# Row sums of an attention inverted and sent to DRAM: eight columns turned by the transfer in place of a turn on TensorE, with one large buffer fewer

## The chip, the core and the metric

The kernel runs on one core of a Trainium2 chip. Five engines work side by side, each through its own instructions in a fixed order: TensorE (PE in the profile, with its weight loads as PEld), VectorE (DVE), ScalarE (ACT), GpSimd (POOL) and SyncE (SP), which here does nothing but issue transfers. An engine waits at an instruction until the semaphores that it needs have been raised by others; what stands behind that instruction waits with it. Transfers (DMAs) between DRAM and the core's memory run beside all of them. The metric is the time of one execution in microseconds on the device.

## What is computed

Two layers of a hybrid encoder over 512 tokens of width 1024. Each layer has a half-step feed-forward block, a mixer and a second feed-forward block, each behind a norm that is shifted and scaled. The mixer holds two attentions, a pooling branch, three gates and an output product. The part that the change touches is the softmax of the two attentions:

```python
def chunked_relpos_attention(q, k, v, gq, gk, rel_bias):
    ...
    p = jax.nn.softmax(logits, axis=-1).astype(v.dtype)
    out = jnp.einsum('bhnqk,bnkhd->bnqhd', p, vb)
...
def forgetting_attention(q, k, v, gq, gk, f_logit):
    ...
        p = jax.nn.softmax(logits, axis=-1).astype(v.dtype)
        return jnp.einsum('bhqk,bkhd->bqhd', p, v)
```

Both have eight heads of 64 columns. The kernel leaves the division by the row sums of the softmax to the end: it weighs the values with the bare exponentials, and multiplies the result by the inverse row sums.

## The kernel before

All products are made in three passes of TensorE with each operand split in a high and a low part (`triple`, lines 119 to 121), so that weights are loaded by SP, split by ScalarE (`hi`, line 272) and VectorE (`lo`, line 274), and only then used.

The code is recorded in one pass. `pe[0]` counts the work given to TensorE so far, in units of a 512-column product; `later(delay, fn)` puts a step on a list that is due when the count has gone on by `delay`, and `poll()`, called before each triple, runs what is due. So the count decides where in the order a step stands. The recorded code then goes through a scheduler, which gives each engine its final order and gives each tile one of the buffers of its tag as these come free. The tag `b` has the largest pool: `NB` buffers of 4 KB in each partition, which serve the activations of the feed-forward blocks, raw weights (line 545), and in the mixer the queries, keys and outputs of the attentions.

`attention` runs for group "a" and then "c", in each of the two layers. Over the heads, four query blocks of 128 rows, taken in three groups:

- `logits` makes the logits in PSUM (line 1021, tag `mm`, four banks shared with other steps), VectorE adds the bias strip and takes the row maximum (line 1027), ScalarE takes the exponential with its row sum (line 1031) into column `odd * 4 + i` of a tile `sums` of 128 rows and 8 columns, one for a pair of heads.
- `turn` turns the exponentials (line 1052), `weigh` multiplies them with the values (line 1079) and adds the two halves into `rows_of[p][:, 0, :]` (lines 1082 and 1083), a `b` tile for each pair of heads whose rows are head columns and whose columns are tokens.
- `send` runs once for each pair, 20 units after the pair's last logits: VectorE inverts the sums (line 1088), TensorE turns the 128 x 8 tile to 8 x 128 (line 1090), ScalarE copies it out of PSUM (line 1092), and GpSimd's queue writes it to DRAM (line 1094), eight rows of 512 bytes.
- `spread`, 24 units later, reads it back with two transfers on GpSimd's queue, each a head's 512 inverse sums given to 64 partitions (line 1100), into `rows_of[p][:, 1, :]`.
- `norm_rows`, 40 units later, multiplies (line 1107) and splits the result for the branch product.

Between these steps a filler hands out triples of the projections or of the gates and branch products, so that TensorE has other work while an attention step waits. GpSimd also prepares the bias strips: a fill of a corner in "a" (line 993), an added mask in "c" (line 1004). There are four pairs, two groups and two layers, so `send` runs 16 times.

Of the kernel before, what the change touches and what calls it, by code (L numbers as in the profile page):

```python
# [15 lines left out]
F32 = mybir.dt.float32  # L16
# [6 lines left out]
P = 128  # L23
# [8 lines left out]
NT = T // P  # L32
# [8 lines left out]
def encoder_kernel(tc, xT, c, w_ada, b_ada, gains, w_gate, w_up, w_down, w_qkv, w_f, w_ubg,  # L41
                   qk_gain, rel, fbias, w_pool, pool_scale, w_branch, w_out, inv_cnt, w_first, out):
    nc = tc.nc
# [11 lines left out]

    mm = nc.tensor.matmul
    uid = [0]
    NB, NRAW = 17, 2

    def nm(s):  # L60
        uid[0] += 1
        return f"{s}_{uid[0]}"

    def st(shape, dt, tag, bufs):
        return sb.tile(shape, dt, tag=tag, bufs=bufs, name=nm(tag))
# [4 lines left out]
    def mmt(shape=(P, T)):  # L70
        return ps.tile(list(shape), F32, tag="mm", bufs=4, name=nm("mm"))
# [13 lines left out]
    pe = [0.0]  # L85
# [12 lines left out]
    def later(delay, fn, group=None):  # L98
        t = Task(pe[0] + delay, fn, group)
        tasks.append(t)  # L100
        return t
# [23 lines left out]
    ident = cp.tile([P, P], F32, name="ident")  # L125
# [49 lines left out]
    inv_dram = {(g, p): dr.tile([2 * NT, P], F32, name=f"inv_dram_{g}{p}") for g in "ac" for p in range(4)}  # L175
# [831 lines left out]
    def attention(qs, ks, vs, strip, ys, filler, budget, group):  # L1007
# [3 lines left out]
        sums, rows_of = {}, {}  # L1011

        def logits(h, group_, strips):
            p, odd = divmod(h, 2)
            (q, ql), k = qs[p], ks[p]
            s, lg, pr = mmt(), t1(T), t2(T)
            at = 0
            for i in group_:
                n = (i + 1) * P
                for z in (q, ql):  # L1020
                    mm(s[:, at:at + n], z[:, odd, i * P:(i + 1) * P], k[:, odd, :n], start=z is q, stop=z is ql)
                at += n
            at = 0
            for i in group_:
                n = (i + 1) * P
                mx = st([P, 1], F32, "mx", 4)
                nc.vector.tensor_tensor_reduce(out=lg[:, at:at + n], in0=s[:, at:at + n], in1=strips[i], scale=-1.0,
                                               scalar=BIG, op0=ALU.add, op1=ALU.min, accum_out=mx)
                if odd == 0 and i == 0:
                    sums[p] = st([P, 2 * NT], F32, "sm", 2)  # L1030
                nc.scalar.activation(pr[:, at:at + n], lg[:, at:at + n], AF.Exp, bias=mx, scale=-1.0,
                                     accum_out=sums[p][:, odd * NT + i:odd * NT + i + 1])
                pe[0] += 0.5 * (i + 1.5)
                at += n
            if odd and i == NT - 1:
                later(LAG_S, lambda: send(p), group)
            later(LAG_T, lambda: turn(h, group_, pr), group)
# [46 lines left out]
            pe[0] += 1.0 * nj  # L1084

        def send(p):
            rs = st([P, 2 * NT], F32, "rs", 1)
            nc.vector.reciprocal(rs, sums[p])
            tp = mmt()
            nc.tensor.transpose(tp[:2 * NT, :P], rs, ident)  # L1090
            flat = st([2 * NT, P], F32, "flat", 1)
            nc.scalar.copy(flat, tp[:2 * NT, :P])
            pe[0] += 0.5
            nc.gpsimd.dma_start(inv_dram[group, p], flat)
            later(LAG_R, lambda: spread(p), group)

        def spread(p):
            for off in range(2):
                r = inv_dram[group, p].rearrange("(h i) q -> h (i q)", h=2)[off:off + 1, :]
                nc.gpsimd.dma_start(rows_of[p][off * HD:(off + 1) * HD, 1, :], r.broadcast_to([HD, T]))  # L1100
            later(LAG_N, lambda: norm_rows(p), group)
# [293 lines left out]
```

## Time and profile before

| | us |
|---|---|
| median of three runs | 2376.86 (2376.07 to 2378.36) |
| the profiled execution, its own time | 2376.93 |
| its span, first to last instruction | 2375.2 |
| TensorE busy | 2356.4 |
| VectorE busy | 1781.1 |
| ScalarE busy | 1164.9 |
| GpSimd busy | 191.4 |

The granted TensorE clock is 1.00 throughout. The attentions run from about 445 to 655 us in the first layer and from about 1620 to 1832 us in the second. In the rows below, a row of the timeline has the start in us, the duration in us, the engine, the line of the code, the operation, the tiles (out<-in, buffer numbers left out), and in square brackets how long the engine stood idle before it and what ended the wait. A row of a group has the count behind an x and then shortest, median and longest duration in ns. A row of the waits has who waited, for whom, the total in us, how often, and the longest. The span of a busy TensorE is modelled: matmuls overlap, so their cost to the engine is the distance from one start to the next.

### The profile page before, as it was taken

The numbers are of one execution on the slowest core, as the hardware profiler recorded it, in microseconds if no ns is written. First come the engines' busy times: TensorE is split into PE (matmuls) and PEld (weight loads), VectorE is DVE, ScalarE is ACT, GpSimd is POOL, SyncE is SP. The second block draws the span as 40 slices with busy tenths as digits, with TensorE's granted clock in tenths as the row PEclk, the third lists the DMA queues.
The fourth block names the chain that finished last, engine by engine and source line by source line (L and its number), as shares of the span: only waits on it lengthen the run. The fifth ranks groups of instructions, "written<-read, shape, count | busy, mean of one in ns | idle before, by whom it ended". The sixth has DMA issues, their size and how long they took to land. (4 is left out here: it accounts for less than half of the span.)

```text
span 2375.2 us, 36712 instructions
## 1 busy us (share of the span) xinstructions
PE 2356.4 (99%) x14172; PEld 2092.2 (88%) x14172; DVE 1781.1 (75%) x3213; ACT 1164.9 (49%) x2048; POOL 191.4 (8%) x309
## 2 busy tenths in 40 slices
PE   8999999999999999999999999999999999999999
PEld 6899998788888898989998999888888888989998
DVE  8889866787668477788678778776866784767784
ACT  5354455676532353544554444556765324544452
POOL 2000002022120000000100000120222101000000
PEclk9999999999999999999999999999999999999999
DMA  7624432333458415244325334423243673223132
GB/s 274 223 91 162 140 128 95 95 98 123 127 188 289 152 63 193 99 143 148 110 89 187 117 115 133 160 89 99 87 138 112 235 258 133 89 98 124 64 116 89
DMA packets 118484, 325.19 MB, mean 137 GB/s; under 512 B 12034, under 2 KB 14338, under 8 KB 118308
## 3 DMA queue, kind: packets, MB, share of 16 engines
q1 hardware_dynamic: 115106, 314.38, 39.1%
q0 software_dynamic: 3200, 8.46, 1.0%
q8 instruction: 111, 1.82, 0.3%
q14 instruction: 65, 0.53, 0.1%
q10 hardware_dynamic: 2, 0.00, 0.0%
HBM read 316.35 MB, written 6.44 MB: 136 GB/s over the span
## 5 line engine op out<-in xcount | busy, mean ns | idle before, releaser
L272 ACT CAST whi<-raw 128x1024 fp32r<-128x1024 f32 (+1 forms) x260 | 270.1, 1043 | 322.4 <-PE acc L120 181.1
L274 DVE TENSOR_TENSOR wlo<-raw,whi 128x1024 fp32r<-128x1024 f32 (+1 forms) x254 | 309.9, 1224 | 156.3 <-ACT whi L272 154.3
L119 PE MATMUL acc<-b,whi 128*128 128x512 f32 (+1 forms) x704 | 262.3, 373 | 0.0
L121 PE MATMUL acc<-b,wlo 128*128 128x512 f32 (+1 forms) x704 | 260.5, 370 | 1.2 <-DVE wlo L274 1.2
L120 PE MATMUL acc<-b,whi 128*128 128x512 f32 (+1 forms) x704 | 260.8, 370 | 0.6 <-DVE b L383 0.6
L119 PE MATMUL mm<-b,whi 128*128 128x256 f32 (+1 forms) x768 | 244.7, 319 | 1.9 <-ACT t L586 1.7
L121 PE MATMUL mm<-b,wlo 128*128 128x256 f32 (+1 forms) x768 | 244.6, 318 | 0.0
L120 PE MATMUL mm<-b,whi 128*128 128x256 f32 (+1 forms) x768 | 244.5, 318 | 0.0
L198 DVE CUSTOM_DVE_ANT_0 v<-v,b,badac 128x1024 f32<-128x1024 f32 x144 | 187.5, 1311 | 20.2 <-DMA v<-in_w_ada_dram 19.9
L119 PE MATMUL mm<-hhi,whi 128*128 128x256 f32 (+1 forms) x616 | 198.8, 323 | 0.4 <-ACT t L586 0.4
L120 PE MATMUL mm<-hlo,whi 128*128 128x256 f32 (+1 forms) x616 | 199.1, 323 | 0.0
L121 PE MATMUL mm<-hhi,wlo 128*128 128x256 f32 (+1 forms) x616 | 199.0, 323 | 0.0
L120 PE MATMUL acc<-hlo,whi 128*128 128x512 f32 x480 | 188.1, 392 | 2.0 <-DVE hlo L790 1.8
L119 PE MATMUL acc<-hhi,whi 128*128 128x512 f32 x480 | 188.0, 396 | 1.0 <-ACT hhi L787 1.0
L121 PE MATMUL acc<-hhi,wlo 128*128 128x512 f32 x480 | 187.6, 391 | 0.0
L382 ACT CAST whi<-raw 128x1024 fp32r<-128x1024 f32 x96 | 100.7, 1049 | 121.3 <-PE mm L120 55.7
L119 PEld LDWEIGHTS mm<-b,whi 128*128 128x128 f32 x768 | 146.3, 190 | 12.4 <-ACT t L586 2.3
L120 PEld LDWEIGHTS mm<-b,whi 128*128 128x128 f32 x768 | 146.3, 191 | 10.3
L121 PEld LDWEIGHTS mm<-b,wlo 128*128 128x128 f32 x768 | 146.3, 190 | 10.2 <-DVE wlo L274 0.3
L121 PEld LDWEIGHTS acc<-b,wlo 128*128 128x128 f32 x704 | 132.6, 188 | 24.4 <-DVE wlo L274 1.6
L120 PEld LDWEIGHTS acc<-b,whi 128*128 128x128 f32 x704 | 132.7, 189 | 23.2 <-DVE b L383 1.4
L119 PEld LDWEIGHTS acc<-b,whi 128*128 128x128 f32 x704 | 132.7, 188 | 21.6
(326 smaller groups left out, 6112.8 us busy)
## 6 DMA issues: line engine op xcount, KB each, us to landing
v<-in_w_ada_dram SPq DMA_DIRECT2D x144, 512.0 KB, 4.8
raw<-in_w_down_dram SPq DMA_DIRECT2D x88, 512.0 KB, 3.8
raw<-in_w_up_dram SPq DMA_DIRECT2D x82, 512.0 KB, 3.6
b<-in_w_gate_dram SPq DMA_DIRECT2D x76, 512.0 KB, 6.3
raw<-in_w_ubg_dram SPq DMA_DIRECT2D x56, 512.0 KB, 4.1
raw<-in_w_qkv_dram SPq DMA_DIRECT2D x42, 512.0 KB, 3.7
raw<-in_w_branch_dram SPq DMA_DIRECT2D x24, 512.0 KB, 3.9
raw<-in_w_out_dram SPq DMA_DIRECT2D x16, 512.0 KB, 3.7
```

The source lines that it names most:

```text
L119: mm(o, lh, rh, start=start, stop=False, skip_group_check=onto)
L120: mm(o, lh, rl, start=False, stop=False, skip_group_check=onto)
L121: mm(o, ll, rh, start=False, stop=stop, skip_group_check=onto)
L198: dot = nc.vector.tensor_tensor_reduce(out=raw, in0=raw, in1=silc[0], scale=1.0, scalar=badac[:, l, j, d:d + 1], op0=ALU.mult, op1=ALU.add ...
L272: nc.scalar.copy(hi, raw)
L274: last["lo"] = lo_eng.tensor_tensor(lo, raw, hi.bitcast(F32), op=ALU.subtract).ins
L382: nc.scalar.copy(hi, src)
```

## The change

`send` no longer turns the tile on TensorE and copies it on ScalarE. The transfer reads the 128 x 8 tile as it is and writes each element to its turned place in DRAM, so that what lands there is the same 8 x 128 block. The tile `rs` has two buffers in place of one, the tile `flat` is gone, the count `pe[0]` no longer goes up by 0.5 in `send`, and the pool of `b` tiles has 16 buffers in place of 17.

```diff
-    NB, NRAW = 17, 2
+    NB, NRAW = 16, 2
...
         def send(p):
-            rs = st([P, 2 * NT], F32, "rs", 1)
+            rs = st([P, 2 * NT], F32, "rs", 2)
             nc.vector.reciprocal(rs, sums[p])
-            tp = mmt()
-            nc.tensor.transpose(tp[:2 * NT, :P], rs, ident)
-            flat = st([2 * NT, P], F32, "flat", 1)
-            nc.scalar.copy(flat, tp[:2 * NT, :P])
-            pe[0] += 0.5
-            nc.gpsimd.dma_start(inv_dram[group, p], flat)
+            with nc.allow_non_contiguous_dma(reason="128 x 8 inverse row sums, turned on their way"):
+                nc.gpsimd.dma_start(inv_dram[group, p].rearrange("j q -> q j"), rs)
             later(LAG_R, lambda: spread(p), group)
```

In the changed code the reciprocal keeps line 1088, the write has line 1090, and the spread has 1096 in place of 1100.

Three places in the orders. The first is TensorE at the first `send` of the first layer, as the difference of the two orders; `rs` is the tile of inverse sums, the `acc` rows are triples of the filler.

```order
 L120 MATMUL acc_4556<-wlo_4675,hhi 128x512
 L121 MATMUL acc_4556<-whi_4674,hlo 128x512
-L1090 MATMUL mm_4816<-ident,rs_4814 8x128
 L119 MATMUL acc_4556<-whi_4680,hhi 128x512
 L120 MATMUL acc_4556<-wlo_4681,hhi 128x512
```

One turn goes, and nothing comes in its place. From here to the end of each mixer's second attention the filler's triples stand one or two steps earlier or later among the attention steps than before; the rows themselves are the same but for the 16 turns.

The second is GpSimd at the last pair of group "a" in the first layer, before:

```order
L1004 TENSOR_TENSOR strip_5684<-strip_5684,cmask 128x128 x3
L1004 TENSOR_TENSOR strip_5870<-strip_5870,cmask 128x128 x3
L1094 DMA inv_dram_a_126<-flat_5764 8x128
L1100 DMA b_5608<-inv_dram_a_126 64x512 x2
L1004 TENSOR_TENSOR strip_5987<-strip_5987,cmask 128x128 x3
L1004 TENSOR_TENSOR ssum_5872<-ssum_5872,cmask 128x128
```

and of the change:

```order
L1004 TENSOR_TENSOR strip_5665<-strip_5665,cmask 128x128 x3
L1004 TENSOR_TENSOR strip_5839<-strip_5839,cmask 128x128 x3
L1090 DMA inv_dram_a_126<-rs_5734 128x8x1
L1004 TENSOR_TENSOR strip_5955<-strip_5955,cmask 128x128 x3
L1096 DMA b_5652<-inv_dram_a_126 64x512 x2
L1004 TENSOR_TENSOR ssum_5841<-ssum_5841,cmask 128x128
```

The three mask steps of a strip for a later head now stand between the write and the spread. On VectorE the multiplication of `norm_rows` for this pair (line 1107) has gone back behind the next two strips' steps of line 1027.

The third is VectorE at the first sum of `weigh` for the third pair of group "a" (heads 4 and 5), with buffer numbers. `b_912` before and `b_914` now are the same tile, `rows_of[2]`. Before:

```order
L289 SCALAR_TENSOR_TENSOR nt_u_895_5269<-nt_q_894_5268,nt_v32_892_5264 128x32
L1083 TENSOR_TENSOR b_912_5319<-mm_913_5320,t1_914_5325 64x256
L290 SCALAR_TENSOR_TENSOR nt_z_896_5270<-nt_u_895_5269,nt_j_893_5266 128x32
L1027 ISA t1_917_5332,mx_919_5338<-mm_916_5331,strip_915_5328 128x128
L1027 ISA mx_919_5338 128x1
```

and of the change:

```order
L1027 ISA t1_923_5372,mx_925_5376<-mm_922_5371,strip_908_5314 128x384
L1027 ISA mx_925_5376 128x1
L1060 TENSOR_TENSOR ptb_906_5304<-mm_921_5364,ptb_906_5304 128x4x128
L1060 TENSOR_TENSOR pta_926_5391<-mm_927_5392,pta_926_5391 128x384
L1083 TENSOR_TENSOR b_914_5330<-mm_915_5331,t1_916_5336 64x256
L1027 ISA t1_929_5402,mx_931_5406<-mm_928_5401,strip_908_5314 128x512
```

The sum has moved from before the first logits of head 5 to just before the last. In the changed program the tile stands in the buffer that held the queries of heads 4 and 5, and waits until the last logits that read them are made; before, it stood in a buffer whose last reader was done. The same holds for the first pair of group "c". On SP, the loads of raw gate weights (line 545) stand in six places behind one or two other loads that they stood ahead of, and in the attentions some strip loads and weight loads have changed places with the load next to them.

## The prediction

> **What bounds the kernel now.** I read the page first, then the windows, then TensorE's waits.
>
> ```profile
> PE 2356.4 (99%) x14172; PEld 2092.2 (88%) x14172; DVE 1781.1 (75%) x3213; ACT 1164.9 (49%) x2048; POOL 191.4 (8%) x309
> ```
>
> TensorE is busy for 2356.4 of 2375.2 us; no other engine comes near. The windows show where the missing 18.8 us are. A row has the window, its length, and the busy time of PE, PEld, DVE, ACT and POOL:
>
> ```profile
> 100.00:150.00 50.00, 50.00 (x336) 46.10 (x335) 49.49 (x76) 25.92 (x40) 0.00 (x0) 1.00 0.38 137
> 500.00:550.00 50.00, 49.29 (x275) 41.14 (x275) 42.33 (x103) 37.95 (x88) 8.28 (x18) 1.00 0.30 94
> 550.00:600.00 50.00, 49.67 (x277) 42.10 (x276) 33.93 (x74) 31.77 (x75) 13.83 (x27) 1.00 0.40 127
> 600.00:650.00 50.00, 49.84 (x274) 42.06 (x273) 31.43 (x68) 28.19 (x63) 9.90 (x22) 1.00 0.37 115
> ```
>
> A feed-forward stretch (the first row) leaves TensorE no idle time at all, and even the three windows of the first attention leave 0.71 + 0.33 + 0.16 = 1.2 us. So the change can gain two things: what TensorE itself spends on the 16 turns, and the few waits that hang on them. Everything off TensorE counts only if it makes TensorE wait. Of all TensorE's waits two belong to `send`:
>
> ```profile
> PE mm L1021 <- ACT flat L1092: 0.7, 2, 0.3
> PE mm L1090 <- DVE b L925: 0.5, 2, 0.2
> ```
>
> In the first, the logits wait for the PSUM bank that the copy to `flat` still holds; in the second the turn itself waits for a bank.
>
> **The turns on TensorE.** One turn takes 270 ns by its own row, but these spans overlap, so I take the distances of the starts:
>
> ```profile
> L1090 PE MATMUL mm<-ident,rs x16: 269/270/273, 473.9 to 1821.6; 128*8 128x128 f32 x16
> 473.67 0.39 PE L121 MATMUL acc<-whi,hlo 128*128 128x512 f32 x1
> 473.90 0.27 PE L1090 MATMUL mm<-ident,rs 128*8 128x128 f32 x1
> 473.93 0.48 PE L119 MATMUL acc<-whi,hhi 128*128 128x512 f32 x1
> 474.24 0.40 PE L120 MATMUL acc<-wlo,hhi 128*128 128x512 f32 x1
> 474.47 0.39 PE L121 MATMUL acc<-whi,hlo 128*128 128x512 f32 x1
> ```
>
> A triple's product starts 0.23 us after the one before (474.24 to 474.47). From 473.67 to 474.24 stand two products and the turn: 0.57 - 0.46 = 0.11 us for the turn. Sixteen of them are 1.8 us. The two waits above, 0.7 + 0.5 = 1.2 us, lose their cause. The next in line for those logits is VectorE, which reads them; I see no row that says it is late there, so I count both in full. Together **-3.0 us**.
>
> ScalarE loses 16 copies of some 0.25 us (4 us in all); it is half idle, and nothing on TensorE is gained by it beyond the bank just counted.
>
> **The write, element by element.** The trace has no transfer of 1024 single elements. The nearest ones, all on GpSimd's queue:
>
> ```profile
> L1094 POOL DMA_DIRECT2D inv_dram_a<-flat x8: 512/512/538, 475.5 to 1729.3; - x8
> DMA to landing us min/median/max: 1.5/2.0/3.1
> L1230 POOL DMA_DIRECT2D x_dram<-xv x8: 563/572/711, 351.2 to 1550.0; - x8
> DMA to landing us min/median/max: 2.9/3.1/3.9
> q0 software_dynamic: 3200, 8.46, 1.0%
> ```
>
> The issue takes 512 ns for 8 rows and 572 ns for the 128 rows of `x_dram`: 0.5 ns a row, so about 1.0 us for 1024 pieces; were it all in proportion to the rows, 8 x 0.57 = 4.6 us. For the landing, the lower end is the 1.5 us of the same 4 KB in eight rows. For the upper end I use the queue's packets: 1.0% of 16 engines' 2375 us is 380 us for 3200 packets, 0.119 us each at 2.6 KB on average; 64 pieces for each of 16 engines would take 7.6 us, on top of 3.1. So 1.5 to 10.7 us; I take **4 us**, nearer the lower end, because the bytes are those of the eight-row write.
>
> The plainest rule against this change is in the Trainium skill, "DMA: Bandwidth & Descriptors", section "Rules for kernel authors": a plain transfer with a rearranged access pattern is no way to turn data, 19 times slower than the chip's own transposing transfer. No run here shows that factor. Taken as 19 times the 2.0 us of the eight-row write it would be an estimate of 38 us, and sixteen of them would come to hundreds of microseconds of late norms.
>
> What hides it is the way from the reciprocal to the norm. The tightest case is the last pair of group "a":
>
> ```profile
> 549.42 0.20 DVE L1088 RECIPROCAL rs<-sm 128x8 f32<-128x8 f32 x1
> 551.68 0.25 ACT L1092 COPY flat<-mm 8x128 f32<-8x128 f32 x1
> 550.43 2.36 POOL L1004 TENSOR_TENSOR strip<-strip,cmask 128x128 f32<-128x128 f32 x3 [8.19 <-DVE b L925]
> 552.75 0.51 POOL L1094 DMA_DIRECT2D inv_dram_a<-flat  x1
> 555.95 1.08 POOL L1100 DMA_DIRECT2D b<-inv_dram_a  x2 [2.69 <-DMA inv_dram_a<-flat]
> 557.84 1.62 POOL L1004 TENSOR_TENSOR strip<-strip,cmask 128x128 f32<-128x128 f32 x3 [0.81 <-DMA strip<-fv_dram]
> 560.89 0.86 DVE L1107 TENSOR_TENSOR b<-b 128x512 f32<-128x512 f32 x1 [1.17 <-DMA b<-inv_dram_a]
> 564.55 0.55 DVE L1027 CUSTOM_DVE_ANT_0 t<-mm,strip 128x384 f32<-128x384 f32 x1
> ```
>
> The sums are inverted at 549.6, yet the write went at 552.75, partly because it waited for the turn and the copy, partly because GpSimd was at a strip until 552.79. In the new order the write still follows that strip, so here it starts no earlier; elsewhere, as at the first pair, it gains what lay between reciprocal and copy (some 3 to 4 us). Behind it now stand the three mask steps, which ran until 557.84 + 1.62 = 559.46 because their strip had to land first. The spread follows at 559.5 in place of 555.95, so **the write may take 559.5 - 552.8 = 6.7 us before it is late by itself**. The spread took 4.9 us to the norm's start, so the norm could start at 564.4. It stands behind line 1027's steps of about 562.6 now, so VectorE waits there about 1.8 us, and the logits' step of 564.55 slips to about 565.1, half a microsecond. VectorE waited before, too:
>
> ```profile
>   DMA b<-inv_dram_c: 8.2, 2
>   DMA b<-inv_dram_a: 1.9, 2
> ```
>
> These are the four waits of line 1107 for the spread, up to 4.1 us each, and among TensorE's waits none names that line. I therefore price half a microsecond of slip on VectorE at nothing on TensorE; without that cover it is 0.5 us in each layer, 1.0 in all.
>
> **Sixteen buffers.** In the feed-forward blocks the loads of raw gate weights are the ones that must now wait for an older tile. The tightest:
>
> ```profile
> 108.71 1.60 SPq L545 DMA_DIRECT2D b<-in_w_gate_dram  x2
> 109.56 0.39 PE L121 MATMUL mm<-b,wlo 128*128 128x512 f32 x1
> 113.56 1.05 ACT L382 CAST ptb<-b 128x1024 fp32r<-128x1024 f32 x1 [0.49 <-DMA b<-in_w_gate_dram]
> 114.99 1.22 DVE L383 TENSOR_TENSOR ptb<-b,ptb 128x1024 fp32r<-128x1024 f32 x1
> 121.38 0.28 PE L119 MATMUL acc<-hhi,ptb 128*128 128x256 f32 x1
> ```
>
> It was issued at 108.71; now it waits for the product that ends at 109.95, 1.24 us later. The cast and the subtraction behind it end at 116.21 and slip to about 117.5, and TensorE needs them at 121.38. The largest slip is that of a load that was issued early:
>
> ```profile
> 192.07 0.90 SPq L545 DMA_DIRECT2D b<-in_w_gate_dram  x2
> 205.15 0.33 SPq L545 DMA_DIRECT2D b<-in_w_gate_dram  x1
> 217.16 1.05 ACT L382 CAST ptb<-b 128x1024 fp32r<-128x1024 f32 x1 [1.05 <-PE acc L121]
> b<-in_w_gate_dram SPq DMA_DIRECT2D x76, 512.0 KB, 6.3
> ```
>
> The second of the two at 192 must now wait for the same step as the one at 205.15, about 12.5 us; with 6.3 us to land it is there by 212, and its first reader runs at 217.16. Its place on SP is now behind two loads that were waiting in the same stretch anyway. Cost: nothing, with 3.9 us to spare at the tightest.
>
> In the attention the third pair's first sum, and that of the first pair of "c", now wait for queries that are still read:
>
> ```profile
> 515.72 0.41 DVE L1083 TENSOR_TENSOR b<-mm,t 64x256 f32<-64x256 f32 x1
> 523.07 0.69 PE L1021 MATMUL mm<-b,b 128*128 128x512 f32 x2
> 525.42 0.27 PE L1052 MATMUL mm<-ident,t 128*128 128x128 f32 x1
> ```
>
> The sum ran at 515.72; now it must wait for the last logits of head 5, which end at 523.76, and ends at 524.2 at the earliest. Until then it holds one of the four PSUM banks and one of two `t1` tiles. The next user of that bank in the new order is the turn that ran at 525.42: about 1.2 us to spare. Queued behind the sum on VectorE is the last strip of the same head, which needs those very logits. So I price it at nothing; if VectorE runs late there, TensorE waits what is missing, and I allow 2 us for each of the four places, 8 us in all.
>
> **Other order.** The filler's triples have moved by one or two. At best all TensorE's idle time of the attentions goes: 2 x 1.2 us, of which 1.2 is counted already, so another -1.2.
>
> **The sum.** The profiled execution took 2376.93 us (span 2375.2), the same as the median 2376.86 within 0.1. 2376.9 - 1.8 - 1.2 = **2373.9 us**, 0.13% faster. About 0.2% (4.8 us) is what a measurement of this kernel can tell from no change: below 2372.1 is faster, above 2381.7 slower.
>
> **The rivals.**
>
> *Nothing is gained, or the banks take it back.* The two waits pass to another release, or the sums that wait for their buffer cost TensorE about what the turns cost it. For it: only 1.2 us to spare at 525.42. Against it: the filler stands between, and the scheduler has put the sum where its buffer comes free. 2376 to 2380, say 2377.
>
> *The element-wise write is the new wait (slower).* The place is the norm on VectorE, in order ahead of the logits' steps; the point is a landing later than 6.7 us. For it: the upper bound is 10.7. Against it: the bytes are few, and VectorE's waits of 4.1 us cost TensorE nothing visible. At 10.7 us the norm is 4.0 us late; if that falls on half of the sixteen sends, 32 us of VectorE's time, and VectorE is busy for 72% of the three windows above (107.7 of 150), TensorE loses 0.72 x 32 = 23 us: 2397. At a landing of 8.5 us it is 10 us: 2384. The Trainium skill's rule on rearranged patterns (above) is this same mechanism taken much further: a landing of 38 us would be 31 us late on all sixteen, an estimate of 360 us. I see nothing in the rows that comes near it, and give it 1 in 100 of this rival's chance.
>
> *The new order suits better.* The idle rest goes as well and a few waits shorter than the rows show: 2373.9 - 1.2 = 2372.7, and with the spread of runs (1 us) just under 2372. For it: the waits exist; against it: there is so little idle time that the order has almost nothing to give.
>
> **How the numbers follow.** Forecast 0.42; nothing gained 0.22; the write late 0.20; the better order 0.16. The better order counts as faster with most of its chance, and the forecast lends a little: 0.18 faster. The write late, with the larger part of the 8 us of the banks: 0.22 slower. Same: 0.60. The range reaches from a little under the better order, 2370.5, to 2386, which holds the write up to a landing of nearly 9 us.
>
> **What would show it.** The turn's line gone from TensorE, its total 1.8 us less busy, and the two rows gone from its waits: the gain. The write's landing in the DMA part: below 6.7 us right, above it a rival. Line 1107's waits for the spread: longer than 10.1 us in all, but without TensorE behind them. TensorE's idle time in 500 to 650 us: about 0.6 us less each layer; if it grows, and line 1052 or 1021 waits for line 1083, it is the buffers. A feed-forward window under 50.00 would prove the load term wrong.

## The result, and the profile after

The changed kernel takes 2449.8 us (2448.7 to 2451.0, four runs) against 2377.6 for the kernel before: a ratio of 1.0304, with an interval of 1.0292 to 1.0316. That is 72 us slower, where 3 us faster was forecast, and far outside the range of 2370.5 to 2386.

The first lines of the page, and windows of the first layer, three of the attention and one of the feed-forward block ahead of it, to set beside those of before (columns as there: the window, its length, busy time of PE, PEld, DVE, ACT and POOL, granted clock, DMA share, GB/s):

```profile
span 2448.7 us, 36723 instructions
PE 2376.4 (97%) x14156; PEld 2103.9 (86%) x14156; DVE 1778.2 (73%) x3213; ACT 1158.5 (47%) x2032; POOL 195.5 (8%) x309
...
500.00:550.00 50.00, 47.66 (x261) 39.48 (x260) 38.79 (x94) 33.98 (x78) 9.14 (x18) 1.00 0.38 93
550.00:600.00 50.00, 41.09 (x223) 34.20 (x222) 27.25 (x66) 25.08 (x62) 12.04 (x21) 0.93 0.39 101
600.00:650.00 50.00, 43.26 (x222) 36.65 (x221) 27.79 (x62) 25.97 (x61) 8.36 (x16) 0.90 0.32 88
100.00:150.00 50.00, 50.00 (x336) 46.08 (x335) 49.30 (x76) 25.77 (x40) 0.00 (x0) 1.00 0.41 137
```

Two things are new. TensorE stands idle for 2448.7 - 2376.4 = 72.3 us, where it was 18.8 before. And it is busy for 20 us more although 16 instructions are gone: the clock that was 1.00 throughout has fallen to 0.90 in the third of these windows. In the fourth, the feed-forward one, TensorE is busy for all of its 50 us, as before: the loads of raw gate weights, which have a buffer fewer, cost it nothing there.

The waits of TensorE and VectorE, the longest rows that were not there before or were much shorter (who waited, for whom, total, times, longest):

```profile
PE mm L1021 <- DVE mx L1027: 30.5, 7, 6.7
PE mm L1052 <- DVE mx L1027: 10.1, 2, 5.7
DVE b L1103 <- DMA b<-inv_dram_c: 65.1, 8, 10.2
DVE b L1103 <- DMA b<-inv_dram_a: 26.1, 7, 9.3
```

Line 1103 (1107 before) is the norm's multiplication. VectorE stands there for 91.2 us, at 15 of the 16 pairs; before it was 10.1 us at four. Behind it in VectorE's order stand the logits' steps of line 1027, and TensorE waits for those.

One pair from end to end, the third of group "c" in the second layer, in the timeline:

```profile
1821.92 0.20 DVE L1088 RECIPROCAL rs<-sm 128x8 f32<-128x8 f32 x1 [0.42 <-ACT t L1031]
1824.05 0.92 POOL L1090 DMA_DIRECT2D inv_dram_c<-rs  x1
1834.91 1.05 POOL L1096 DMA_DIRECT2D b<-inv_dram_c  x2 [9.22 <-DMA inv_dram_c<-rs]
1843.07 0.69 DVE L1103 TENSOR_TENSOR b<-b 128x512 f32<-128x512 f32 x1 [8.98 <-DMA b<-inv_dram_c]
1844.49 1.01 PE L1021 MATMUL mm<-b,b 128*128 128x384 f32 x2 [5.47 <-DVE mx L1027]
1845.30 0.63 PE L119 MATMUL acc<-b,whi 128*128 128x512 f32 x1
1845.72 0.63 PE L120 MATMUL acc<-b,whi 128*128 128x512 f32 x1
1846.15 0.63 PE L121 MATMUL acc<-b,wlo 128*128 128x512 f32 x1
```

The write is issued at 1824.05 and the spread can follow only at 1834.91. It needs another 8.2 us to the norm. VectorE has stood for 8.98 us by then and TensorE for 5.47, and the products that come next start 0.42 us apart, not 0.23. The windows of the same stretch show why:

```profile
1826.00:1834.00 8.00, 8.00 (x45) 6.80 (x44) 6.05 (x11) 5.25 (x10) 0.00 (x0) 1.00 0.11 12
1836.00:1842.00 6.00, 3.02 (x18) 2.34 (x16) 0.00 (x0) 0.00 (x0) 1.26 (x3) 1.00 0.99 288
1843.00:1846.00 3.00, 1.51 (x4) 1.42 (x5) 2.22 (x7) 1.85 (x7) 0.47 (x1) 0.50 0.00 0
```

While the write is on its way, **all transfers together move 12 GB/s**. Weight loads are issued into this window at 1828.14 and 1831.68, and one of them lands 10.9 us after its issue. Then what was held up comes at once, at 288 GB/s, and the spread has to share with it. When TensorE can go on, its clock is granted at 0.50.

The landing of the write (first line below), of the spread (second), and of the weight loads of line 261 between 545 and 690 us (third), each as shortest, median and longest:

```profile
DMA to landing us min/median/max: 9.7/11.1/11.6
DMA to landing us min/median/max: 3.0/6.0/7.5
DMA to landing us min/median/max: 3.5/6.2/9.0
```

Before they were 1.5/2.0/3.1, 2.7/3.2/5.7 and 3.4/3.9/4.5. Yet the transfer engines do little for the write. GpSimd's queue has as many packets as before, and its share has gone from 1.0% to

```profile
q0 software_dynamic: 3200, 8.46, 1.4%
```

which is 34 in place of 24 us for each engine (1.4% of 2449, 1.0% of 2375). The write of the pair above is 16 packets of 256 bytes in the trace, 0.40 to 0.49 us each, and all of them are over by 1826.4. In the 4.6 us from there on no packet of any queue starts (second row):

```profile
1825.60:1826.40 0.80, 0.80 (x6) 0.62 (x5) 0.43 (x1) 0.78 (x2) 0.09 (x1) 1.00 0.59 5
1826.40:1831.00 4.60, 4.60 (x26) 3.90 (x25) 3.65 (x6) 3.19 (x6) 0.00 (x0) 1.00 0.00 0
```

So most of the 10 us come behind the packets, in a time for which the profile counts no work of these engines.

### The profile page after: what moved, and what is told of

The parts are those of the page before. It is cut to its first block, busy times and chain, and to the rows that moved or that the text cites. A ratio compares the mean times of both kernels' runs of the same rounds, so it can differ in the third digit from the quotient of the medians.

```text
span 2448.7 us, 36723 instructions
## 1 busy us (share of the span) xinstructions
PE 2376.4 (97%) x14156; PEld 2103.9 (86%) x14156; DVE 1778.2 (73%) x3213; ACT 1158.5 (47%) x2032; POOL 195.5 (8%) x309
## 4 chain that ended last, share of the span: by engine, by line
PE 80%; DMA 8%; DVE 5%; issue 3%; ACT 3%; POOL 2%; DVEq 0%; SPq 0%; ACTq 0%; POOLq 0%
PE acc L119 16%; PE acc L120 16%; PE acc L121 16%; PE mm L119 10%; PE mm L121 10%; PE mm L120 10%; DMA b<-inv_dram_c 2%; DMA inv_dram_a<-rs 1%; DMA b<-inv_dram_a 1%; DMA inv_dram_c<-rs 1%; PE mm L1021 1%; POOL strip L1141 1%; ACT whi L272 1%; PE mm L1079 1%; DVE v L198 1%
## 5 line engine op out<-in xcount | busy, mean ns | idle before, releaser
L119 PE MATMUL acc<-b,whi 128*128 128x512 f32 (+1 forms) x704 | 265.1, 377 | 0.2 <-ACT b L382 0.2
L120 PE MATMUL acc<-b,whi 128*128 128x512 f32 (+1 forms) x704 | 264.3, 375 | 0.2 <-DVE b L383 0.2
```

Of the source, the lines that this page charges most:

```text
L119: mm(o, lh, rh, start=start, stop=False, skip_group_check=onto)
L120: mm(o, lh, rl, start=False, stop=False, skip_group_check=onto)
```

## The experiments

### The buffers: the change with 17, and before with 16

```diff
-    NB, NRAW = 16, 2
+    NB, NRAW = 17, 2
```

in the change, and the reverse in the kernel before.

> The change with 17 buffers of tag b kept. Theory L (the element-wise write makes its own pair late: it lands after some 11 us, the spread and the norm come late, VectorE stands at the norm with the next logits behind it): about 2450 us, within 5 of the changed kernel. Theory S (the write holds up every other transfer for some 10 us, so that strips and weights are late as well as the spread): the same, about 2450. Theory B (the sixteenth buffer and the order that it brings are what cost): 2374 to 2380.

> The kernel before, turn and copy kept, with 16 buffers of tag b. Theories L and S: within 4 us of before, as the prediction priced the buffers at nothing with up to 8 us allowed. Theory B: most of the 72 us, 2430 or more.

The change with 17 buffers took 2428.4 us, 1.0207 (1.0186 to 1.0228) of before; the kernel before with 16 took 2379.9, 1.0002 (0.9992 to 1.0013). Sixteen buffers cost nothing by themselves, and theory B falls. But with the element-wise write the 17 buffers are 21 us better, which no theory expected: the write lands in 9.9 us by the median, and VectorE waits at the norm for 57.6 + 21.2 us in place of 91.2. The order differs between the two in many places, so this may be the place where a stop of the transfers falls and not the buffer; which of the two was not tried.

### A write that nobody waits for, in three forms

The kernel before, with one more write behind each norm, read by nothing. Its turn, copy and eight-row write are untouched. First with single elements, dense in DRAM:

```diff
             split_to(y[:, 0, :], y[:, 1, :], full)
+            with nc.allow_non_contiguous_dma(reason="read by nothing"):
+                nc.gpsimd.dma_start(spare[group, p].rearrange("j q -> q j"), y[:, 0, :2 * NT].bitcast(F32))
```

> The kernel before with one more element-wise write of 128 x 8 to turned places for each of the 16 pairs, into DRAM that nobody reads, from the norm's result, so that it starts when its own pair's chain is done. Theory L: nothing waits for these writes, so 2376 to 2383. Theory S: the transfers of all queues move next to nothing for about 9 us behind each of them, the strip and weight loads issued then land 5 to 9 us later than in before, and the time rises by 20 to 70 us: 2397 to 2447.

Then the control, the same 4 KB as eight rows:

```diff
+            nc.gpsimd.dma_start(spare[group, p], y[:2 * NT, 0, :P].bitcast(F32))
```

> The control for the spare write: the same place, the same tile, the same 4 KB, but as 8 rows of 512 bytes. Theory S (the single elements stop the other transfers): 2376 to 2384, loads land in their usual 3.5 to 4.5 us. Theory Q (GpSimd's queue pays, because its instruction waits for the norm's result with the strips and the next pair's write behind it): the 52 us of the spare element-wise write come again, 2420 to 2435.

And last, when the forms below had been seen, the same 1024 elements with 64 bytes from one to the next (theories G and N are told with the forms: G has elements that share a line of 64 bytes written one after the other, N has the number of pieces count):

```diff
+                nc.gpsimd.dma_start(spare[group, p][:, :, 0].rearrange("j q -> q j"), y[:, 0, :2 * NT].bitcast(F32))
```

> The spare write of single elements again, from the same place and tile, but with 64 bytes from one element to the next in DRAM: as many pieces, none beside another. Theory G: a stop of some 3 us in place of 9, which the loads' lead mostly covers: 2380 to 2395. Theory N: as the dense spare write, 2425 to 2440.

| spare write | us | ratio to before (interval) | its landing, us |
|---|---|---|---|
| 1024 elements, dense | 2431.7 | 1.0217 (1.0202 to 1.0233) | 9.4/10.1/12.2 |
| 8 rows of 512 bytes | 2379.9 | 1.0000 (0.9990 to 1.0010) | 1.5/2.0/4.4 |
| 1024 elements, 64 bytes apart | 2376.6 | 0.9998 (0.9989 to 1.0007) | 3.0/3.4/4.5 |

Dense elements cost 52 us though nothing waits for them. The control excludes GpSimd's queue (theory Q): the instruction stands at the same place and waits for the same tile, and in all three kernels the other instructions of every engine stand in the same order as before. The third row has as many elements and the same issue time (0.92 us), and is free. Its 16 packets take as long as those of the dense write (0.49 us at most in both); behind the last of them it lands within 0.7 to 1.5 us, and the dense write, where its landing could be read, 6.0 to 8.4 us later. The window from about 4 to 8 us behind the first spare write, in the kernels with dense elements, with rows, and with elements apart:

```profile
494.50:498.50 4.00, 4.00 (x27) 3.48 (x26) 2.83 (x7) 2.76 (x8) 2.51 (x4) 1.00 0.14 15
494.60:498.60 4.00, 4.00 (x27) 3.48 (x25) 2.84 (x7) 2.77 (x8) 1.79 (x3) 1.00 0.48 152
496.20:500.20 4.00, 4.00 (x27) 3.49 (x26) 2.82 (x7) 2.76 (x8) 2.50 (x4) 1.00 0.50 144
```

The same loads are due at this place in all three: 15 GB/s in the first, 144 to 152 in the others. In the dense version TensorE waits behind VectorE and for weights, and VectorE for spreads that a stop holds up though their own write has eight rows:

```profile
PE mm L1022 <- DVE ptb L1061: 20.9, 11, 4.3
PE acc L119 <- ACT whi L273: 8.6, 4, 4.5
DVE b L1108 <- DMA b<-inv_dram_c: 43.7, 8, 6.8
```

This is theory S: the write stops the transfers of others. In the changed kernel the write also stands in its own pair's chain, as theory L has it; how the 72 us divide between the two was not measured.

### The change with a write that is not turned

```diff
-                nc.gpsimd.dma_start(inv_dram[group, p].rearrange("j q -> q j"), rs)
+                nc.gpsimd.dma_start(inv_dram[group, p].rearrange("j (a b) -> (j a) b", b=2 * NT), rs)
```

> The change with its 4 KB written as they lie, 128 rows of 32 bytes one behind the other, not turned (so the inverse sums that are read back belong to other rows). All else is the change. If the forecast's sum without the write is right (1.8 us of turns and 1.2 us of waits off TensorE): 3 us under before, about 2374 to 2377 where before is at 2377 to 2380. If the 16 buffers or the order cost something in the change: 2382 or more. If the wait for a write from 128 rows is a cost by itself: over 2390.

It took 2375.6 us, 0.9992 (0.9982 to 1.0001) of before. The instructions of all engines stand in the same order as in the change, so its profile is the change without the stop:

```profile
span 2371.5 us, 36723 instructions
PE 2353.0 (99%) x14156; PEld 2091.5 (88%) x14156; DVE 1777.9 (75%) x3213; ACT 1160.0 (49%) x2032; POOL 191.4 (8%) x309
DMA to landing us min/median/max: 1.7/1.8/3.5
DVE b L1103 <- DMA b<-inv_dram_a: 4.7, 2, 2.4
```

The third line is the landing of the write of 128 rows, the fourth VectorE's waits at the norm. Against the change the span is 2448.7 - 2371.5 = 77.2 us shorter. TensorE's idle time is 18.5 in place of 72.3 us, 53.8 less, and its busy time 2353.0 in place of 2376.4, 23.4 less for the same instructions: **the dense elements cost 54 us of waiting and 23 us of lower clock**.

### The norm later, and the write on another queue

```diff
-    LAG_T, LAG_V, LAG_S, LAG_R, LAG_N = 30, 20, 20, 24, 40
+    LAG_T, LAG_V, LAG_S, LAG_R, LAG_N = 30, 20, 20, 24, 80
```

> The change with the norm recorded 40 units (about 9 us) later, so that VectorE meets it when the spread has landed. Theory L: nearly all is regained, 2376 to 2395 (the last pair of each group is fetched early by the branch product and stays late). Theory S: the norm's waits go, but strips and weights still land late: 2400 to 2440.

2430.1 us, 1.0200 (1.0182 to 1.0218). It agrees with theory S by its number, but it is no test: the scheduler put the norm back to the same place in VectorE's order (two of the 16 stand one step earlier), and VectorE still waited there for 56.2 + 18.3 us. As with the 17 buffers, some 20 us are gained with small changes in the order of every engine; which of them gains it is open.

```diff
-                nc.gpsimd.dma_start(inv_dram[group, p].rearrange("j q -> q j"), rs)
+                nc.sync.dma_start(inv_dram[group, p].rearrange("j q -> q j"), rs)
```

> The change with its element-wise write issued by SP in place of GpSimd. If the stop comes from the single elements, whoever issues them: the other transfers stop for 9 us again, 2430 to 2460. If it comes from the way GpSimd's queue makes its descriptors: the write lands in 2 to 4 us, and the time is 2372 to 2385.

2405.8 us, 1.0110 (1.0091 to 1.0129): between the two that were expected. The write on SP's queue lands after

```profile
DMA to landing us min/median/max: 8.3/8.7/10.9
```

and the stop is there: below, the same weight load in this kernel, issued 1.7 us behind such a write, and in the one whose write is not turned, each for 6 us from about 1.3 us behind the load's issue.

```profile
530.00:536.00 6.00, 6.00 (x31) 5.00 (x31) 4.49 (x12) 3.77 (x11) 0.00 (x0) 1.00 0.21 29
527.80:533.80 6.00, 6.00 (x31) 5.02 (x31) 4.50 (x13) 3.76 (x11) 0.52 (x2) 1.00 0.35 126
```

29 GB/s in place of 126: whoever issues the write, it stops the others, and GpSimd's queue is not the cause. The write starts earlier (at once behind the reciprocal, without GpSimd's strips ahead of it) and lands 2.4 us sooner by the medians; VectorE's waits at the norm fall from 91.2 to 39.9 + 15.9 = 55.8 us. That fits a loss of 26 in place of 72 us, but how much of it is the earlier start and how much the order was not separated.

### Which writes stop the others

Three kernels, each the kernel before with spare writes in other forms, one form for each pair of a layer; each kernel ran once.

```diff
+            o, s = {("a", 0): lambda: (d, z[:8, :P]),
+                    ("a", 1): lambda: (d, z[:, :8]),
+                    ("a", 2): lambda: (d.rearrange("a q b -> q a b"), z[:, :8].rearrange("q (a b) -> q a b", b=2)),
...
+                nc.gpsimd.dma_start(o, s)
```

> The kernel before with spare writes in seven forms, one for each pair: 8 rows of 512 bytes, 128 rows of 32 bytes, 256 pieces of 16, 512 of 8, 1024 of 4 (each of these turned in DRAM), 1024 of 4 with 64 bytes from one to the next, and 512 of 4. If the count of pieces sets the stop at some 9 ns each: about 9 us for 1024, 4.5 for 512 of either size, 2.3 for 256, 1.2 for 128, and the spaced ones like the dense ones. If it is that neighbours in DRAM share a line which is read and written again: the spaced form stops nothing and the dense ones do. If it is the element size below some bound alone: a step between two forms, not a line.

> The kernel before with spare writes of 1024 elements of 4 bytes whose neighbours in DRAM lie 8, 16, 32, 64 and 128 bytes apart, and of 128 and 256 elements that lie dense (one and two columns). Theory G (elements that share a line of 64 bytes are written one after the other, some 0.5 us each): the dense ones stop the transfers for 8 us though they are few; 8 bytes apart about 4 us, 16 apart about 2, and from 64 up no difference, the 2 to 3 us that 1024 pieces take in any case. Theory N (the number of pieces counts): the 128 and 256 dense ones stop for 1 to 2 us, and the 1024 take as long at every distance.

> The kernel before with spare writes of 4-byte elements, one form for each pair: dense columns of 16, 32, 64 and 128 elements from as many partitions; 128 elements 8 bytes apart; and 1024 elements, of which the eight of a partition lie dense, in pairs with 8 bytes between the pairs, or 8 bytes apart. Theory W (what stops the transfers are elements beside each other that come from different partitions): dense columns stop them even when few, for longer the more there are; the three forms by partition and the column 8 bytes apart stop nothing and land in 2 to 4.5 us. Theory D (any two elements of 4 bytes that lie side by side): the dense form by partition and the pairs stop them too, for some 7 us, and the forms 8 bytes apart do not.

For the eight of a partition every second element of the tile is read, so that elements that lie side by side in DRAM are still written one by one. Landing in the two layers:

| form | us | form | us |
|---|---|---|---|
| 8 rows of 512 bytes | 1.8, 1.6 | 1024 elements turned, dense | 8.7, 11.2 |
| 128 rows of 32 bytes | 2.2, 2.3 and 1.7, 1.7 | 512 turned, dense | 9.9, 9.4 |
| 256 pieces of 16 bytes, turned | 1.9, 3.3 | 256 turned, dense | 9.4, 9.2 |
| 512 pieces of 8 bytes, turned | 4.0, 4.1 | one column of 128, dense | 7.2, 7.2 and 7.8, 8.2 |
| 1024 elements turned, 8 bytes apart | 3.8, 4.2 and 3.8, 4.4 | one column of 64, dense | 6.1, 6.5 |
| the same, 16 apart | 4.2, 4.2 | one column of 32, dense | 5.5, 5.2 |
| the same, 32 apart | 3.3, 3.9 | one column of 16, dense | 1.6, 2.7 |
| the same, 64 apart | 3.2, 3.2 and 4.1, 5.1 | eight of a partition, dense | 7.6, 8.2 |
| the same, 128 apart | 4.5, 4.5 | eight of a partition, in pairs | 7.7, 5.6 |
| one column of 128, 8 apart | 6.4, 5.4 | eight of a partition, 8 apart | 5.2, 7.0 |

The count does not set it: 256 dense elements take as long as 1024, while 1024 elements 8 bytes apart are done in 4 us (theory N falls). A shared line of 64 bytes does not set it either: eight elements in a line are about as quick as one (theory G falls, which wanted 4 us of stop at 8 bytes apart). It needs no neighbours from different partitions: the dense form by partition is slow as well (theory W falls). What stays is that single elements of 4 bytes laid side by side land late from 32 of them on, and that a gap of 4 bytes between them is enough for 1024 in the turned form. Theory D, any two side by side, fits the dense forms and the pairs, but not the 5 to 7 us of the last row, 8 bytes apart.

Part of that row is another wait. The landing is counted from the issue, and the packets of the column 8 bytes apart begin only 3.5 and 3.2 us behind it, with loads under way. From the end of its packets it lands in 2.4 and 1.7 us, the dense column of 128 in 5.9 to 6.9. Counted so, the eight of a partition take 5.4 and 6.0 us dense, 4.7 and 2.7 in pairs and 2.6 and 4.6 when 8 bytes apart, which theory D still does not give.

Nor does every late landing stop the others. From about 2 us behind the issue, with the dense column of 128 and, at the same place, with 128 rows of 32 bytes; then with 256 dense elements and, at their place, with 256 pieces of 16 bytes:

```profile
589.20:593.20 4.00, 4.00 (x25) 3.45 (x24) 1.88 (x5) 2.55 (x7) 0.00 (x0) 1.00 0.44 132
589.50:593.50 4.00, 4.00 (x25) 3.45 (x24) 1.88 (x5) 2.55 (x7) 1.15 (x3) 1.00 0.40 140
612.70:618.70 6.00, 6.00 (x34) 5.04 (x33) 2.81 (x6) 3.52 (x8) 0.00 (x0) 1.00 1.24 16
613.00:619.00 6.00, 6.00 (x34) 5.04 (x33) 2.81 (x6) 3.51 (x8) 1.29 (x3) 1.00 0.38 109
```

The column lets 132 GB/s through where 140 moved, though it lands after 7.2 us itself; the 256 elements leave 16 of 109. The same stretch as above, 4 to 8 us behind the first spare write, with elements 8 bytes apart (turned) and with the dense form by partition:

```profile
494.50:498.50 4.00, 4.00 (x26) 3.48 (x25) 2.80 (x7) 2.77 (x8) 2.48 (x4) 1.00 0.48 152
495.30:499.30 4.00, 4.00 (x27) 3.48 (x26) 2.78 (x7) 2.76 (x8) 2.46 (x4) 1.00 0.21 23
```

So the condition is narrowed down and its mechanism stays open.

### The turn on VectorE

The gain that was forecast, taken in another way: VectorE turns blocks of 32 x 32. First in four steps into a tile whose eight rows are written as before:

```diff
+            nc.vector.reciprocal(wide[:, :2 * NT], sums[p])
+            flat = st([32, P], F32, "flat", 1)
+            for z in range(4):
+                nc.vector.transpose(flat[:, 32 * z:32 * z + 32], wide[32 * z:32 * z + 32, :])
+            nc.gpsimd.dma_start(inv_dram[group, p], flat[:2 * NT, :])
```

> The turn made on VectorE, in four blocks of 32 x 32 into the tile flat, and written as eight rows of 512 bytes as before; no turn on TensorE, no copy on ScalarE, 17 buffers. If the gain that was forecast for the change is real without its write: 2373 to 2376 against 2377 of before, at the edge of what can be told apart. If VectorE's four more steps cost as much as TensorE gets: no change.

Then in one step, with four writes of eight rows of 128 bytes:

```diff
+            flat = st([P, 32], F32, "flat", 1)
+            nc.vector.transpose(flat, wide)
+            for z in range(4):
+                nc.gpsimd.dma_start(inv_dram[group, p][:, 32 * z:32 * z + 32], flat[32 * z:32 * z + 2 * NT, :])
```

> The turn made by one VectorE step on 128 x 32 (four blocks turned in place) and written by four transfers of eight rows of 128 bytes; no turn on TensorE, no copy on ScalarE, 17 buffers. If the steps on VectorE were what took the gain back in the version with four blocks (five steps of 0.2 us for each pair, two here): 1 to 3 us under before. If there is no gain to be had: the same as before.

With four steps: 2382.3 us, 1.0010 (0.9999 to 1.0020), no gain. One step of 32 x 32 takes as long as the reciprocal of all 128 rows:

```profile
L1092 DVE STREAM_TRANSPOSE flat<-wide x64: 191/200/204, 471.5 to 1822.1; 32x32 f32<-32x32 f32 x64
```

so each pair costs VectorE 4 x 0.20 = 0.8 us more than before, ahead of the logits. That this took the gain back is likely and not shown: in the profiled execution TensorE also ran at a clock of 0.50 from 1488.4 to 1495.3 us, outside the attentions. With one step: **2373.2 us, 0.9987 (0.9978 to 0.9996) of before**, some 3 us less. The interval leaves out no change only just, and 0.13% is less than the 0.2% that the prediction wanted to see.

```profile
span 2370.7 us, 36788 instructions
PE 2352.6 (99%) x14156; PEld 2091.7 (88%) x14156; DVE 1783.0 (75%) x3229; ACT 1159.8 (49%) x2032; POOL 210.8 (9%) x358
```

TensorE is busy for 3.8 us less than before, and the time shows no harm from the three writes more on GpSimd's queue.

## Why the prediction was wrong, step by step

- **TensorE sets the time; idle time of the others is free.** Right, and it is how the loss shows: only the 54 us for which TensorE itself waits count of VectorE's 91, and then the clock.
- **The turns, 1.8 us, and two waits, 1.2 us.** Their sum is borne out within the interval, the two terms are not one by one. In the version that is not turned the turn's line and both waits are gone, and TensorE is busy for 2356.4 - 2353.0 = 3.4 us less, more than the 1.8; but its idle time is 18.5 us after 18.8, so that other waits have taken the place of most of the 1.2. Its time is 1.9 us less by the ratio, with an interval from 4.3 less to 0.2 more; the version with one step on VectorE shows 3.1 us less (1.0 to 5.2).
- **The write lands in about 4 us.** This is the step that failed. It was taken "nearer the lower end, because the bytes are those of the eight-row write"; measured is 9.7 to 11.6 us with a median of 11.1. The same bytes land in 1.8 us as 128 rows of 32 bytes, in 3.4 us as 1024 elements apart, and in 10 as 1024 dense elements: the form sets it, not the bytes and not the count. The upper end of 10.7 us came near only by accident. It took each element for a packet of 0.119 us; the queue has 3200 packets as before, the write is 16 of them, and most of its time comes behind them.
- **The price of a late write: 4.0 us late on half of the sends, times 0.72, 23 us.** The place was right (VectorE at the norm, the logits behind it). The point of 6.7 us from which it decides was not tested, since every landing lay above it. But even at the upper end the sum gave 2397, and 2450 was measured. Three parts were missing. VectorE waits for 91.2 / 15 = 6.1 us at 15 sends, not 4.0 at eight, because the spread lands late as well, in the burst that follows. All other loads stop with the write; in the kernel before, such writes for which nothing waits cost 52 us. And TensorE's clock falls at each of its ten waits of 2.3 to 6.7 us, 23 of the 77 us.
- **Sixteen buffers at nothing.** Right by themselves (1.0002). Beside the stops the two numbers of buffers differ by 21 us, in a way that the prediction had no term for.
- **The rival "element-wise write late" with 0.20.** The right one, too low in price and in chance. The sentence from the Trainium skill (page "DMA: Bandwidth & Descriptors", section "Rules for kernel authors") pointed the right way, and I gave it 1 in 100 of that rival. What it compares, a rearranged pattern with the transposing transfer, no run here shows; against the eight-row write, to which the prediction applied the factor of 19, it is 11.1 to 2.0 us, a factor of 5.5.

## What to carry to other kernels

A small transfer is priced by its form, not by its bytes, and where the trace has no transfer of that form, what it does to all other transfers belongs into the range as well as its own landing. Do not write single 4-byte elements densely into DRAM; turn the data on an engine, or write rows. When a wait grows to several microseconds on TensorE, add what the lower clock behind it costs.

## What the chip showed that was not expected

A write of 4 KB in 1024 dense elements holds up the transfers of both queues for some 8 us, whether GpSimd issues it (15 GB/s where 144 to 152 were due) or SP (29 where 126 were due). Most of that time lies behind the write's own packets. The Trainium skill, page "DMA: Bandwidth & Descriptors", section "Specifications", says that transfers need at least 512 bytes for full rate, since the engine reads and writes back below that. The runs show that this size is not where the stop begins: rows of 32 bytes landed in 1.8 us and stopped nothing.

TensorE's clock fell to 0.50 at a wait of 5.47 us (the window from 1843 us), and its products then started 0.42 us apart. The Trainium skill, page "TensorE: Matmul & The Clock Gate", section "What's actually happening", gives half rate after an idle window of about 3.4 us; the trace agrees in the rate. In the length it does not: three of the ten waits at which the clock fell were 2.3 to 2.7 us long, shorter than that window.
